# Conformer layer on one core: first weights ahead of x, a head first in the mixer, later half's norms in pieces, four one-pair weight blocks to a tile

## The chip, the cores and the metric

The kernel runs on one core of a Trainium2 chip. The metric is device time in microseconds of one execution, the median of several runs. The engines are named as the profile names them: PE is TensorE's matmuls, PEld its weight loads, DVE is VectorE, ACT is ScalarE, POOL is GpSimd and SP is SyncE, whose queue issues every DMA here. Each engine works through its own queue in order; a wait of one instruction holds up all behind it on that engine.

## The reference

One layer for 1,056 tokens (1,024 of a new stream and 32 of a running one), model width 1,024, in float32:

```
x = x + 0.5 * RMSNorm_post(SwiGLU_1(RMSNorm_pre(x)))
h = RMSNorm_pre(x); p = h @ w_in
conv group: GLU -> causal depthwise conv (width 31) -> LayerNorm -> swish
ret group:  rotary q,k -> chunkwise retention (4 heads of 128) -> GroupNorm -> * swish(g)
x = x + RMSNorm_post(concat(conv, ret) @ w_out)
x = x + 0.5 * RMSNorm_post(SwiGLU_2(RMSNorm_pre(x)))
```

The feed-forward width is 2,816; w_in has 3,072 columns (four convolution blocks of value and gate, four heads of q, k, v, g, 128 columns each). The outputs are y and the new convolution and retention states.

## The kernel before

**Arithmetic.** Each operand of a large product is split into a high part (rounded to fp32r) and a low part (the rest), and a product takes three matmuls: high by high, high by low, low by high. A weight split is one copy on ACT (L146, tile `whi`) and one subtraction, on POOL as a rule (L147, tile `wlo`). Tokens lie along the free axis in two halves of 528, each in two pieces of Q = 264; features lie on the 128 partitions. Pairs of feature blocks and token pieces form 2x2 block products. The feed-forwards mostly do these with seven block products in place of eight (`visit`, L305 to 348, matmul L323), with sums and differences of blocks as operands; elsewhere plain blocks are used (`visit_plain`, L266 to 303, matmul L275).

**Units.** `program` is a list of units. A unit is one block of weights with one or two visits (one for each half that uses it). `prep` (L156 to 208) is a generator for its weights: it fetches four blocks into `raw` tiles (five buffers), then forms sums and differences on DVE, then splits (seven buffers each of `whi` and `wlo`). `run` (L358 to 402) goes through the units; while the products of one are issued, it steps the generator of the next, and when a unit ends it issues the fetch of the unit after the next.

**Order.** There is a planned clock, `now`, which advances by 0.124 us for each large matmul issued (L278, L326). Side work is put into a heap with a due time (`later`, `at`), and is issued when the clock reaches it. Instructions that come out this way are then placed in the engines' queues by the tile framework, with a simulated timeline. So the constants on L49 to L58 set where norms, convolution taps and retention steps fall among the matmuls.

**Stages.** First the opening: vec, both halves of x (16 loads, L976), two constant tiles, and `begin(0)` (L983 to 989), which squares and sums x (`Norm`, L406 to 456), scales it (L475) and splits it. The first half's statistics are a matmul `sp` (L437), `v` on DVE (L440), a power on POOL (L441) and a matmul `bc` (L449); the squares go through one buffer, tag `sq` (L415). The feed-forward's up part (L524 to 597) follows: three pairs of units for the first half alone with plain blocks, three for the second half alone, and the rest for both. Hidden values are stored to DRAM in split form (L559, L560) and loaded again (L113) for the down part, which runs over five blocks of pairs, `DBLK` = 1, 2, 2, 2, 4 pairs; the first four use the kind `paired` with seven products, the last is plain, first half and then second.

**Kind `paired`** (L178 to 195). It puts two 128-column-by-nk blocks side by side into each of four `raw` tiles, so a unit has four fetches, four DVE operations and four splits. With nk = 1 the splits are 256, 256, 256 and 128 wide, with nk = 2 twice that.

**Between feed-forward and mixer.** After the last visit of a half, `post_norm` (L506 to 520) scales ys (L512), adds the residual (L513), stores, and starts the next `pre_norm` (L467 to 495), which scales again (L475) and splits (`tplain`, L242 to 248, DVE at L247). In both, all four pairs are issued in one go.

**Mixer.** Twenty-four plain units, twelve for a half: a convolution is one unit (`cu`), a head is two (`hu`: q and k, then v and g). The order in a half is c0, c1, h0, c2, h1, c3, h2, h3. A convolution's 31 taps are DVE instructions on 558 or 528 columns (L740, L742), one a planned us, and the four convolutions of a half queue behind each other. A head's q and k are multiplied by a cosine table out of PSUM (L836). Retention runs in five chunks a head and a half (`retain`, L856 to 925) with three steps each; `RET_DELAY` holds the delay from the first step to the second, from the second to the third, from the unit to the first chunk, and between chunks. Results of convolutions and heads go through DRAM (`cd`, `rd`), and `conv_norm` and `ret_build` make the operands of the out-projection from them, after the last unit of the half. Feed-forward hidden blocks (`h`), results (`ys`), convolutions (`cu`) and heads (`hd`) share four buffers, tag `f`. PSUM has four banks for large products: two `px`, one `py`, one `pz`. The out-projection has four plain units for the first half, then four for the second, and is followed by the second feed-forward.

Of the kernel before, what the change touches and what calls it, by code (L numbers as in the profile page):

```python
# [10 lines left out]
F32 = mybir.dt.float32  # L11
# [4 lines left out]
P = 128  # L16
# [34 lines left out]
TAP_STEP = 1.0  # L51
RET_DELAY = (4.0, 10.0, 4.0, 4.0)
NORM_DELAY = (2.0, 3.0)
BEGIN_DELAY = 2.0
SPILL_STEP = (1.4, 2.8, 5.6, 9.0)
# [9 lines left out]
def layer_kernel(ctx: ExitStack, tc: tile.TileContext, a: dict, o: dict):  # L65
# [90 lines left out]
    def prep(src, nk, kind, dve_lo):  # L156
# [20 lines left out]

        def paired():  # L178
            n = nk * P
            r = [raw() for _ in range(4)]  # L180
            a11, s1, a12, s2, s4, a22, s3 = (r[p // 2][:, p % 2 * n:p % 2 * n + n] for p in range(7))
            for t, i in ((a11, 0), (s3, 1), (a22, 2), (a12, 3)):
                fetch(t, src, i, nk)
            yield
            v = nc.vector
            v.tensor_tensor(s1, s3, a22, ALU.add)
            v.tensor_tensor(s2, s1, a11, ALU.subtract)
            v.tensor_tensor(s4, a12, s2, ALU.subtract)  # L188
            v.tensor_tensor(s3, a11, s3, ALU.subtract)
            yield  # L190
            for p in range(4):
                m = n if p == 3 else 2 * n
                hi, lo = split(r[p], m, p in dve_lo)
                ws.extend((hi[:, o:o + n], lo[:, o:o + n]) for o in range(0, m, n))
                yield
# [11 lines left out]

        return ws, {"seven": seven, "paired": paired, "plain": plain}[kind]()

# [147 lines left out]

    def run():  # L358

        made = [prep(s, nk, kind, dl) for s, nk, _, dl, kind in program]  # L360
        made.append(([], iter(())))
        next(made[0][1])
        for _ in made[0][1]:
            pass
        next(made[1][1])
        for n, (src, nk, visits, _, kind) in enumerate(program):
# [4 lines left out]
            if n + 1 < len(program):  # L371
                nkind = program[n + 1][4]
                pieces_ = {"seven": 7, "paired": 4, "plain": 4}[nkind]

                if nkind == kind == "seven":
                    plan = [max(0, total - 8 - (total > 7) * 3)] + [total - 7 + i for i in range(7)]
                else:
                    plan = [0] + [total - 1 - (pieces_ - 1 - i) * max(1, min(2, (total - 1) // pieces_)) for i in range(pieces_)]
            else:
                plan = []  # L380
# [25 lines left out]
    class Norm:  # L406
# [4 lines left out]

        def add(self, x, dt=0.0):

            def first():
                sq = fp.tile([P, 4, Q], F32, name=nm("sq"), tag="sq", bufs=1)  # L415
                nc.scalar.activation(sq, x, AF.Square)
# [49 lines left out]

    def pre_norm(j, bs, nrm, g, dst, also=None, plain=False, dt=NORM_DELAY, then=lambda: None):  # L467

        def done(rb):
            if also is not None:  # L470
                ex = [tp.tile([P, 4, Q], F32R, name=nm("ex"), tag=t) for t in ("tbh", "tbl")]
            rest = []
            for kp, b in enumerate(bs):
                for i, x in enumerate(pieces(b)):
                    nc.vector.scalar_tensor_tensor(x, x, col(g, 2 * kp + i), rb, ALU.mult, ALU.mult)  # L475
                if plain:
                    tplain(b, dst, j, kp)
                    continue
                if kp % 2 == 0:
# [25 lines left out]

    def post_norm(j, fs, nrm, xs, g, mul, out, gpre, dst, also=None, plain=False):  # L506

        def done(rb):
            n2 = Norm(4)
            for kp, b in enumerate(groups(fs)):  # L510
                for k, y in zip((2 * kp, 2 * kp + 1), pieces(b)):
# [3 lines left out]
                if gpre is not None:  # L515
                    n2.add(b, POST_STEP * (kp + 1))
            if gpre is not None:
                pre_norm(j, groups(fs), n2, gpre, dst, also if j == 0 else None, plain, NEXT_DELAY)

        nrm.finish(1.0 / D, mul, done)  # L520

    def ffn(xt, wgu, wdn, res, gpost, out, gpre, nxt, lead, first):  # L524
# [114 lines left out]
        for b, (k0, nk) in enumerate(DBLK):  # L639
            last = b == len(DBLK) - 1  # L640

            def dn_visit(m, j, before, b=b, last=last):
# [9 lines left out]
                def after():  # L652
                    if last:
# [4 lines left out]
                        if m == 3:  # L658
                            post_norm(j, ys[j], sums[j], xs[j], gpost, 0.5, out, gpre, nxt, None, True)

# [10 lines left out]
            if last:  # L671
                for j in (0, 1):
                    for m in range(4):
                        unit(src[m], nk, [dn_visit(m, j, None)], (), "plain")
            else:
                for m in range(4):
                    unit(src[m], nk, [dn_visit(m, j, start if m == j == 0 else None) for j in (0, 1)], (), "paired")

# [299 lines left out]

    inp = [[fetch_x(j, q) for q in (0, 1)] for j in (0, 1)]
    nc.sync.dma_start(out=idn, in_=a["idn"])  # L980
    nc.sync.dma_start(out=msk, in_=a["msk"])

    def begin(j):  # L983
        bs = groups(inp[j])
        nrm = Norm(4)
        for i, b in enumerate(bs):
            nrm.add(b, 0.0 if j == 0 else 2.0 * i)
        pre_norm(j, bs, nrm, "f1pre", xt[0], first[0] if j == 0 else None, False, (0.0, 0.0) if j == 0 else (10.0, 3.0),
                 (lambda: later(BEGIN_DELAY, lambda: begin(1))) if j == 0 else lambda: None)

    begin(0)
    ffn(xt[0], a["wgu1"], a["wd1"], a["x"], "f1post", x1, "mpre", xt[1], 3, first[0])
# [10 lines left out]
    for j in (0, 1):  # L1003
        cu(0, j)
        cu(1, j)
        hu(0, j)
        cu(2, j)
        hu(1, j)
        cu(3, j)
        hu(2, j)  # L1010
        hu(3, j)
        src, nk, ((b, tj, dst, acc, after),), dl, pl = program[-1]
# [7 lines left out]
    ffn(xt[3], a["wgu2"], a["wd2"], x2, "f2post", o["y"], None, None, 3, first[1])  # L1020
    run()
    flush()
# [65 lines left out]
```

## Time and profile before

| | |
|---|---|
| median of 3 runs | 2114.32 us (2112.15 to 2115.62) |
| the profiled execution | 2111.57 us, span of its instructions 2109.8 us |
| PE busy | 1927.7 us, 91% |
| DVE busy | 1441.4 us, 68% |
| POOL busy | 995.5 us, 47% |
| ACT busy | 825.8 us, 39% |
| HBM read and written | 217.54 MB and 88.50 MB, 145 GB/s over the span |
| TensorE's granted clock, mean | 0.974 |

How to read it: matmuls are pipelined and their ends are modelled, so a busy PE need not be at its peak; the count of matmuls in a stretch tells more. A row of waits gives who waited, for whom, the us in total, the number of waits and the longest. A row of groups gives line, engine, operation, tiles and shapes, then the busy time, the mean of one in ns, and the idle time before them with what ended it. The feed-forwards fill about 40 to 800 us and 1320 us to the end; the mixer lies between.

### The profile page before, as it was taken

To read this page: it belongs to the slowest core of one execution; us is meant where nothing else is said; L and a number is where in the kernel's file an instruction comes from. 1 tells how busy PE (TensorE), PEld (TensorE's weight loads), DVE (VectorE), ACT (ScalarE), POOL (GpSimd) and SP (SyncE) were. 2 spreads that over 40 slices of the span, in tenths; PEclk is the share of its full clock that TensorE was granted. 3 is DMA by queue.
4 is the path that set the end of the run, shared out by engine and by line. 5 is a ranking of instruction groups with operands and counts; after the bars stand their busy time and mean duration, and the time that the engine had idled before them with its cause. 6 is when DMAs were issued, how large, how long until landed. Compare 5 with 4: busy or idle time off the path is not lost. (4 is left out here: it accounts for less than half of the span.)

```text
span 2109.8 us, 39258 instructions
## 1 busy us (share of the span) xinstructions
PE 1927.7 (91%) x15272; PEld 1886.6 (89%) x15272; DVE 1441.4 (68%) x2386; ACT 825.8 (39%) x1564; POOL 995.5 (47%) x734
## 2 busy tenths in 40 slices
PE   4988999999899997589988999888999999999995
PEld 4988999999899997589988999887999999889995
DVE  7777566543677378989799855988676544477545
ACT  5444444444322233233433345444444444432221
POOL 2556544454354454354454446456554545344441
PEclk9999999999999999699999999999999999999998
DMA  4354434433975653032332354324444423676742
GB/s 146 104 175 146 141 117 151 135 102 122 329 256 165 214 163 113 23 94 87 105 104 80 99 188 130 127 81 163 140 157 155 135 86 130 233 256 222 254 142 83
DMA packets 143977, 308.60 MB, mean 146 GB/s; under 512 B 17456, under 2 KB 47536, under 8 KB 143792
## 3 DMA queue, kind: packets, MB, share of 16 engines
q1 hardware_dynamic: 143792, 306.10, 43.7%
q8 instruction: 120, 1.97, 0.4%
q14 instruction: 65, 0.53, 0.1%
HBM read 217.54 MB, written 88.50 MB: 145 GB/s over the span
## 5 line engine op out<-in xcount | busy, mean ns | idle before, releaser
L147 POOL TENSOR_TENSOR wlo<-raw,whi 128x512 fp32r<-128x512 f32 (+1 forms) x620 | 874.7, 1427 | 885.5 <-ACT whi L146 714.1
L146 ACT ACTIVATE whi<-raw 128x512 fp32r<-128x512 f32 (+1 forms) x632 | 366.3, 606 | 652.2 <-issue 178.1
L742 DVE SCALAR_TENSOR_TENSOR cu<-cu,vec 128x558 f32<-128x558 f32 (+1 forms) x240 | 242.9, 1032 | 1.6
L275 PE MATMUL px<-tbh,whi 128*128 128x264 f32 x768 | 225.9, 294 | 19.4 <-DVE hd L836 14.3
L323 PE MATMUL px<-tbh,whi 128*128 128x264 f32 x832 | 238.8, 287 | 3.1 <-ACT h L313 1.9
L323 PE MATMUL px<-tbh,wlo 128*128 128x264 f32 x832 | 237.2, 285 | 0.0
L323 PE MATMUL px<-tbl,whi 128*128 128x264 f32 x832 | 236.7, 284 | 0.0
L275 PE MATMUL px<-tbl,whi 128*128 128x264 f32 x768 | 221.5, 289 | 0.6 <-DVE tbl L247 0.6
L275 PE MATMUL px<-tbh,wlo 128*128 128x264 f32 x768 | 221.4, 288 | 0.0
L275 PEld LDWEIGHTS px<-tbh,whi 128*128 128x128 f32 x768 | 147.6, 192 | 20.3 <-issue 14.5
L323 PEld LDWEIGHTS px<-tbh,whi 128*128 128x128 f32 x832 | 157.2, 189 | 5.2 <-ACT h L313 2.8
L323 PEld LDWEIGHTS px<-tbh,wlo 128*128 128x128 f32 x832 | 157.3, 189 | 0.0
L323 PEld LDWEIGHTS px<-tbl,whi 128*128 128x128 f32 x832 | 157.2, 189 | 0.0
L275 PEld LDWEIGHTS px<-tbl,whi 128*128 128x128 f32 x768 | 147.1, 192 | 0.9 <-DVE tbl L247 0.9
L275 PEld LDWEIGHTS px<-tbh,wlo 128*128 128x128 f32 x768 | 147.1, 191 | 0.1
L316 DVE TENSOR_TENSOR h<-h,px 128x264 f32<-128x264 f32 x152 | 59.1, 424 | 117.1 <-PE px L323 109.7
L323 PE MATMUL px<-tah,whi 128*128 128x264 f32 x416 | 119.8, 288 | 14.2 <-ACT whi L146 13.3
L323 PE MATMUL py<-tbh,whi 128*128 128x264 f32 x416 | 121.9, 293 | 9.5 <-DVE h L316 7.6
L323 PE MATMUL pz<-tbh,whi 128*128 128x264 f32 x416 | 121.6, 292 | 8.1 <-DVE ys L316 3.3
L323 PE MATMUL pz<-tbl,whi 128*128 128x264 f32 x416 | 119.5, 287 | 7.1 <-DVE tbl L237 6.3
L323 PE MATMUL pz<-tah,wlo 128*128 128x264 f32 x416 | 119.8, 288 | 4.7 <-DVE wlo L147 2.9
L323 PE MATMUL py<-tah,whi 128*128 128x264 f32 x416 | 120.5, 290 | 2.7 <-ACT ys L313 1.0
(217 smaller groups left out, 6023.6 us busy)
## 6 DMA issues: line engine op xcount, KB each, us to landing
raw<-in_wgu SPq DMA_DIRECT2D x224, 256.0 KB, 3.3
hth<-hh SPq DMA_DIRECT2D x28, 924.0 KB, 4.0
htl<-hl SPq DMA_DIRECT2D x28, 924.0 KB, 5.0
raw<-in_win SPq DMA_DIRECT2D x96, 256.0 KB, 3.3
tbh<-hth SPq DMA_DIRECT2D x44, 528.0 KB, 5.6
tbl<-htl SPq DMA_DIRECT2D x44, 528.0 KB, 6.0
raw<-in_wd SPq DMA_DIRECT2D x64, 256.0 KB, 3.0
raw<-in_wd SPq DMA_DIRECT2D x96, 128.0 KB, 3.1
```

Source lines behind the costliest of these rows:

```text
L146: nc.scalar.activation(hi, x[:, :n], AF.Copy)
L147: (nc.vector if dve else nc.gpsimd).tensor_tensor(lo, x[:, :n], hi, ALU.subtract)
L275: mm = nc.tensor.matmul(ps, l[:, w], r, start=k == 0 and i == 0 and n == 0, stop=k == nk - 1 and i == 1 and n == 2)
L316: nc.vector.tensor_tensor(to, to, ps, ALU.add)
L323: mm = nc.tensor.matmul(ps, l[:, w], r, start=start and k == 0 and i == 0, stop=k == nk - 1 and i == 2, skip_group_check=True)
L742: nc.vector.scalar_tensor_tensor(cc, u[:, t:t + m], vec[:, w + t:w + t + 1], cc, ALU.mult, ALU.add)
```

## The change

1. **Opening.** x is no longer loaded before the program is built. `run` fetches the first unit's four weight blocks, then calls `opening`, which loads the first half of x and the identity, and puts two things into the heap: `begin(0)`, and after it `others`, which loads the second half of x and the mask. Between them the splits of the first unit and the fetch of the second unit are issued. `begin(0)` squares into two tiles of tag `g` instead of the single `sq` buffer. `BEGIN_DELAY`, from the first half's scaling to `begin(1)`, goes from 2 to 8.
2. **Packing.** `paired` becomes `packed`: 4 // nk blocks to a `raw` tile. For nk = 2 it is as before; for nk = 1 four blocks share a tile, so the seven fill two tiles and the splits are 512 and 384 wide.
3. **Mixer's order.** In the first half h0, c0, c1, h1, c2, h2, c3, h3; the second half is as before.
4. **Later half's norms.** Between the first feed-forward and the mixer, the second half's `post_norm` and `pre_norm` issue their four pairs `SPREAD` = 5 planned us apart, with delays of 4 and 4 in the first and 20 and 4 in the second.
5. **Retention.** `RET_DELAY` goes from (4, 10, 4, 4) to (6, 11, 4, 5).

```diff
-RET_DELAY = (4.0, 10.0, 4.0, 4.0)
+RET_DELAY = (6.0, 11.0, 4.0, 5.0)
+SPREAD = 5.0
-BEGIN_DELAY = 2.0
+BEGIN_DELAY = 8.0
...
-        def paired():
+        def packed():
             n = nk * P
-            r = [raw() for _ in range(4)]
-            a11, s1, a12, s2, s4, a22, s3 = (r[p // 2][:, p % 2 * n:p % 2 * n + n] for p in range(7))
+            per = 4 // nk
+            r = [raw() for _ in range((6 + per) // per)]
+            a11, s1, a12, s2, s4, a22, s3 = (r[p // per][:, p % per * n:p % per * n + n] for p in range(7))
...
-            for p in range(4):
-                m = n if p == 3 else 2 * n
-                hi, lo = split(r[p], m, p in dve_lo)
+            for p, x in enumerate(r):
+                m = min(per, 7 - p * per) * n
+                hi, lo = split(x, m, p in dve_lo)
...
-    def run():
+    def run(opening):
         made = [prep(s, nk, kind, dl) for s, nk, _, dl, kind in program]
         made.append(([], iter(())))
         next(made[0][1])
+        opening()
         for _ in made[0][1]:
             pass
         next(made[1][1])
...
-                pieces_ = {"seven": 7, "paired": 4, "plain": 4}[nkind]
+                pieces_ = {"seven": 7, "packed": (7 * program[n + 1][1] + 3) // 4, "plain": 4}[nkind]
...
     def pre_norm(...):
...
             for kp, b in enumerate(bs):
+                if slow:
+                    later(SPREAD * kp, lambda kp=kp, b=b: scaled(kp, b))
+                    continue
+                scaled(kp, b)
...
     def post_norm(...):
...
                 if gpre is not None:
-                    n2.add(b, POST_STEP * (kp + 1))
+                    n2.add(b, 1.5 if slow else POST_STEP * (kp + 1))
+            for kp, b in enumerate(groups(fs)):
+                if slow:
+                    later(SPREAD * kp, lambda kp=kp, b=b: pair(kp, b))
+                else:
+                    pair(kp, b)
             if gpre is not None:
-                pre_norm(j, groups(fs), n2, gpre, dst, also if j == 0 else None, plain, NEXT_DELAY)
-        nrm.finish(1.0 / D, mul, done)
+                pre_norm(j, groups(fs), n2, gpre, dst, also if j == 0 else None, plain,
+                         (4 * SPREAD, 4.0) if slow else NEXT_DELAY, slow=slow)
+        nrm.finish(1.0 / D, mul, done, (4.0, 4.0) if slow else NORM_DELAY)
...
-    inp = [[fetch_x(j, q) for q in (0, 1)] for j in (0, 1)]
-    nc.sync.dma_start(out=idn, in_=a["idn"])
-    nc.sync.dma_start(out=msk, in_=a["msk"])
+    inp = [None, None]
+    def opening():
+        inp[0] = [fetch_x(0, q) for q in (0, 1)]
+        nc.sync.dma_start(out=idn, in_=a["idn"])
+        at(0.0, lambda: begin(0))
+        at(0.0, others)
+    def others():
+        inp[1] = [fetch_x(1, q) for q in (0, 1)]
+        nc.sync.dma_start(out=msk, in_=a["msk"])
...
+        if j == 0:
+            sq = [gtile("sq"), gtile("sq")]
...
     for j in (0, 1):
-        cu(0, j)
-        cu(1, j)
-        hu(0, j)
-        cu(2, j)
-        hu(1, j)
-        cu(3, j)
-        hu(2, j)
-        hu(3, j)
+        for x in ("h0", "c0", "c1", "h1", "c2", "h2", "c3", "h3") if j == 0 else ("c0", "c1", "h0", "c2", "h1", "c3", "h2", "h3"):
+            (cu if x[0] == "c" else hu)(int(x[1]), j)
```

More of the change, by code (lines that the diff above doesn't have):

```diff
@@ L206, in plain @@
                 yield
-        return ws, {"seven": seven, "paired": paired, "plain": plain}[kind]()
+        return ws, {"seven": seven, "packed": packed, "plain": plain}[kind]()
     PART = ((0, 0), (1, 0), (0, 1), (1, 1), (0, 2), (1, 3), (1, 2))
@@ L410, in __init__, with add, first @@
             self.n, self.got = n, 0
-        def add(self, x, dt=0.0):
-            def first():
-                sq = fp.tile([P, 4, Q], F32, name=nm("sq"), tag="sq", bufs=1)
+        def add(self, x, dt=0.0, sq=None):
+            def first(sq=sq):
+                if sq is None:
+                    sq = fp.tile([P, 4, Q], F32, name=nm("sq"), tag="sq", bufs=1)
                 nc.scalar.activation(sq, x, AF.Square)
@@ L465, in groups, with pre_norm @@
         return [f[:, 4 * i:4 * i + 4] for f in fs for i in (0, 1)]
-    def pre_norm(j, bs, nrm, g, dst, also=None, plain=False, dt=NORM_DELAY, then=lambda: None):
+    def pre_norm(j, bs, nrm, g, dst, also=None, plain=False, dt=NORM_DELAY, then=lambda: None, slow=False):
         def done(rb):
@@ L472, in done, with scaled @@
             rest = []
-            for kp, b in enumerate(bs):
+            def scaled(kp, b):
                 for i, x in enumerate(pieces(b)):
@@ L477, in done @@
                     tplain(b, dst, j, kp)
+            for kp, b in enumerate(bs):
+                if slow:
+                    later(SPREAD * kp, lambda kp=kp, b=b: scaled(kp, b))
+                    continue
+                scaled(kp, b)
+                if plain:
                     continue
@@ L504, in residual, with post_norm, pair @@
         return xs
-    def post_norm(j, fs, nrm, xs, g, mul, out, gpre, dst, also=None, plain=False):
+    def post_norm(j, fs, nrm, xs, g, mul, out, gpre, dst, also=None, plain=False, slow=False):
         def done(rb):
             n2 = Norm(4)
-            for kp, b in enumerate(groups(fs)):
+            def pair(kp, b):
                 for k, y in zip((2 * kp, 2 * kp + 1), pieces(b)):
@@ L658, in after @@
                         if m == 3:
-                            post_norm(j, ys[j], sums[j], xs[j], gpost, 0.5, out, gpre, nxt, None, True)
+                            post_norm(j, ys[j], sums[j], xs[j], gpost, 0.5, out, gpre, nxt, None, True, j == 1 and gpre is not None)
                 return (before, hts[b][j], evict if last else dst, not last and b > 0, after)
@@ L676, in ffn @@
                 for m in range(4):
-                    unit(src[m], nk, [dn_visit(m, j, start if m == j == 0 else None) for j in (0, 1)], (), "paired")
+                    unit(src[m], nk, [dn_visit(m, j, start if m == j == 0 else None) for j in (0, 1)], (), "packed")
     def mixer(xt, wt):
@@ L985, in begin @@
         nrm = Norm(4)
+        if j == 0:
+            sq = [gtile("sq"), gtile("sq")]
         for i, b in enumerate(bs):
-            nrm.add(b, 0.0 if j == 0 else 2.0 * i)
+            nrm.add(b, 0.0 if j == 0 else 2.0 * i, sq[i // 2][:, 4 * (i % 2):4 * (i % 2) + 4] if j == 0 else None)
         pre_norm(j, bs, nrm, "f1pre", xt[0], first[0] if j == 0 else None, False, (0.0, 0.0) if j == 0 else (10.0, 3.0),
                  (lambda: later(BEGIN_DELAY, lambda: begin(1))) if j == 0 else lambda: None)
-    begin(0)
     ffn(xt[0], a["wgu1"], a["wd1"], a["x"], "f1post", x1, "mpre", xt[1], 3, first[0])
@@ L1020, in layer_kernel @@
     ffn(xt[3], a["wgu2"], a["wd2"], x2, "f2post", o["y"], None, None, 3, first[1])
-    run()
+    run(opening)
     flush()
```

## The prediction

> **What bounds the kernel now.** I read the page first, then TensorE's waits, then a table of windows.
>
> ```profile
> span 2109.8 us, 39258 instructions
> PE 1927.7 (91%) x15272; PEld 1886.6 (89%) x15272; DVE 1441.4 (68%) x2386; ACT 825.8 (39%) x1564; POOL 995.5 (47%) x734
> ```
> ```profile
> PE sp L437 <- DVE ss L420: 36.3, 5, 16.1
> PE px L275 <- DVE hd L836: 14.3, 1, 14.3
> PE px L323 <- ACT whi L146: 13.3, 9, 2.9
> PE pz L275 <- DVE ex L485: 8.3, 2, 5.7
> ```
> ```profile
> 500.00:525.00 25.00, 25.00 (x208) 25.00 (x207) 8.31 (x18) 11.50 (x24) 10.94 (x9) 1.00 0.33 107
> 25.00:50.00 25.00, 15.82 (x109) 14.93 (x110) 25.00 (x38) 11.37 (x17) 6.06 (x4) 1.00 0.17 58
> 525.00:575.00 50.00, 42.73 (x308) 39.88 (x308) 29.90 (x74) 21.87 (x57) 19.36 (x23) 0.97 0.89 316
> 825.00:875.00 50.00, 17.54 (x120) 16.86 (x120) 50.00 (x69) 15.67 (x24) 14.00 (x8) 0.66 0.27 87
> 800.00:1212.00 412.00, 351.97 (x2738) 341.07 (x2738) 376.31 (x628) 148.93 (x316) 187.24 (x143) 0.93 0.29 88
> 1018.00:1212.00 194.00, 175.19 (x1372) 169.72 (x1371) 183.55 (x324) 74.57 (x161) 90.05 (x70) 0.96 0.31 91
> 1825.00:1875.00 50.00, 41.96 (x305) 39.13 (x304) 30.69 (x77) 20.65 (x53) 17.10 (x20) 0.97 0.88 323
> ```
>
> After the length, the columns are PE, PEld, DVE, ACT and POOL with counts, then TensorE's clock, DMA share and GB/s. TensorE is the bound almost everywhere: 208 matmuls in 25 us, 0.120 us each, is its full rate. It falls short in the opening (109 in 25 us), in each feed-forward's one-pair blocks (308 and 305 in 50 us, against 416), and where the mixer begins (120 in 50 us). In the mixer's projections, 800 to 1212, VectorE is busy 376 of 412 us, so there are nearly two bounds at once. The change reaches all four places. Where TensorE is the bound on both sides of a stall, what is taken out of the stall goes into the end time.
>
> **The opening.** DMA rates of the first 60 us in 40 slices of 1.5 us, then instructions from the timeline (start, length, engine, line, what it did, and in brackets the idle time before it and what ended that):
>
> ```profile
> GB/s 0 131 334 306 374 394 372 371 367 366 371 388 138 0 15 160 171 178 157 161 153 154 75 0 0 0 0 0 0 11 0 0 0 0 0 141 40 86 203 214
> ```
> ```profile
> x<-in_x SPq DMA_DIRECT2D x16, 264.0 KB, 5.3
> ```
> ```profile
> 13.50 1.08 ACT L416 ACTIVATE sq<-x 128x1056 f32<-128x1056 f32 x1 [1.57 <-DVE ss L420]
> 16.13 1.92 PE L437 MATMUL sp<-one,ss 128*88 128x1 f32 x12 [16.13 <-DVE ss L420]
> 19.63 11.43 POOL L147 TENSOR_TENSOR wlo<-raw,whi 128x512 fp32r<-128x512 f32 x7
> 24.78 9.56 DVE L475 SCALAR_TENSOR_TENSOR x<-x,vec,ss 128x528 f32<-128x528 f32 x8
> 35.70 0.59 PE L275 MATMUL pz<-ex,whi 128*128 128x264 f32 x1 [5.70 <-DVE ex L485]
> 859.67 5.51 DVE L475 SCALAR_TENSOR_TENSOR ys<-ys,vec,ss 128x528 f32<-128x528 f32 x8
> ```
>
> One square buffer makes ACT and DVE take turns: 1.08 + 1.57 = 2.65 us a round, until the sum is ready at 16.13. Two tiles with four halves end the turns, but four weight loads of 256 KB (1.05 MB at the row's 372 GB/s, 2.8 us) now go ahead of x. By that row the first 2.3 MB, which hold the first half of x (8 x 264 KB), are in by 9.0 us, so now by about 12; a square (1.08), its adds (about 1.5) and landing follow: the sum at about 15, a gain of 1. The larger part is the scaling, L475: 9.56 us beside the POOL splits that start at 19.63, and 5.51 for the same eight instructions near 860. With weights first, these splits run while x lands, so 4 us go. The second half's squares and adds, now queued behind, no longer sit ahead of the scaling: 1 more. So the first dense matmuls move from 35.7 to about 29.7: **-6**. Bounds: -2 if the next unit's splits still meet the scaling, -9 if the 5.70 us wait for the low part shrinks as well. The second half of x is moved behind the second unit's weights on SP's queue, whose issues wait for raw buffers. Its reader is the first seven-product unit, six units (6 x 96 x 0.120 = 69 us) later: that cover pays for it, and for a beginning of the second half that is 6 us later (BEGIN_DELAY).
>
> **One-pair blocks.** The waits of TensorE in 520 to 600 and in 1822 to 1900, SP's own wait in 1822 to 1880, and the splits by shape:
>
> ```profile
> PE px L323 <- ACT whi L146: 4.3, 3, 2.3
> PE px L323 <- ACT whi L146: 5.5, 3, 2.9
> SPq L154 <- DVE raw L189: 8.8, 4, 4.0
> L147 POOL TENSOR_TENSOR wlo<-raw,whi 128x256 fp32r<-128x256 f32 x14 | 11.2, 815 | 33.4 <-ACT whi L146 33.4
> L147 POOL TENSOR_TENSOR wlo<-raw,whi 128x512 fp32r<-128x512 f32 x6 | 8.2, 1395 | 6.3 <-ACT whi L146 5.2 <-PE pz L323 1.0
> ```
>
> A unit has 42 matmuls, 5.0 us, and takes four of five raw buffers, so its successor's loads wait until they are free. With two buffers a unit the successor's loads go out while it runs. The splits fall from four to two: 3 x 0.815 and a smaller one become 1.395 and a smaller one, about 0.6 us of POOL less a unit, off the path. At most 4.3 + 5.5 = 9.8 us go, 12 with the low clock behind such stops (0.97 in both windows). But DMA is 0.89 and 0.88 busy there, and what is late next is the stored hidden values of the next block on the same queue, or the first, longer split (+0.58). I take about 60%: **-6** (0 to -12).
>
> **The mixer's beginning.**
>
> ```profile
> 851.20 1.92 PE L437 MATMUL sp<-one,ss 128*88 128x1 f32 x12 [14.94 <-DVE ss L420]
> 856.00 2.87 PE L449 MATMUL bc<-idn,r 88*128 88x88 f32 x12 [2.88 <-POOL r L441]
> 873.18 0.56 PE L275 MATMUL px<-tbh,whi 128*128 128x264 f32 x1 [14.31 <-DVE hd L836]
> ```
> ```profile
> 853.99 5.76 DVE L742 SCALAR_TENSOR_TENSOR cu<-cu,vec 128x558 f32<-128x558 f32 x8
> 870.74 1.25 DVE L247 TENSOR_TENSOR tbl<-ys,tbh 128x1056 fp32r<-128x1056 f32 x1
> 872.62 0.42 DVE L836 TENSOR_TENSOR hd<-px,cos 128x264 f32<-128x264 f32 x1
> 893.74 6.90 DVE L742 SCALAR_TENSOR_TENSOR cu<-cu,vec 128x558 f32<-128x558 f32 x4
> ```
> ```profile
> L742 DVE SCALAR_TENSOR_TENSOR cu<-cu,vec 128x558 f32<-128x558 f32 (+1 forms) x240 | 242.9, 1032 | 1.6
> ```
> ```profile
> 893.12 6.91 POOL L147 TENSOR_TENSOR wlo<-raw,whi 128x512 fp32r<-128x512 f32 x4
> 1000.00:1025.00 25.00, 25.00 (x205) 24.41 (x204) 15.48 (x42) 10.46 (x25) 12.20 (x12) 1.00 0.39 117
> 1212.00:1262.00 50.00, 50.00 (x421) 49.87 (x419) 28.86 (x69) 26.13 (x51) 24.07 (x21) 1.00 0.60 196
> ```
>
> TensorE stands 14.94 + 2.88 + 14.31 = 32.1 us, and about 3 more go to the low clock (0.66): 35. Both long waits have one cause, the later half's norms among convolution taps. First its statistics come late; then the head's tile (third of four in tag "f", after two convolutions) can only be had when the last of that half's ys is read (870.74), and L836 follows at 872.62. Now a head comes first, with no taps, and the third tile is asked for after three units, 34.6 us. By the constants the norms, five us apart, free their tiles 37 and 47 us after they begin, and a unit can fill four banks, 11.5 us, before its tile must be there. I expect at most a few us of this stop to stay. What is moved with it: the first head issues its cosine and sine loads a unit after the norms instead of three units later, and the same 11.5 us of banks cover their landing; the later half's eight output stores are spread with its pairs, and each waits on SP for VectorE ahead of weight loads that are needed one unit, 11.5 us, later. Both at nothing; without that cover a late load would cost what it lacks, which the bounds below hold.
>
> What is left is VectorE's work, of which nothing is removed. It was idle 412 - 376 = 36 us. By the constants (96 x 0.124 = 11.9 a unit) the first half's 124 taps ran from 11.9 to 135.9 of 142.8; now from 35.7 to 159.7, so 17 taps pass into the second half. They fill the hole between the halves (idle 25 - 15.5 = 9.5 us at 1000 to 1025). Another 12 us can lag past 1212, where VectorE works 29 of 50 us. So 9.5 + 12 = 21.5: **-22**, and 390 us for this stage. Bounds: -35, the whole stop, and 0, where the taps take it all back. The longer retention delays (+2, +1, +1 a chunk) take small waits off TensorE here, and where VectorE is the bound that is worth nothing. I leave them at 0, within the bounds.
>
> **The mixer's end.** The last head, and the window after it:
>
> ```profile
> 1256.21 0.33 DVE L916 SCALAR_TENSOR_TENSOR hd<-rp,vec,hd 128x105 f32<-128x105 f32 x1 [3.46 <-PE rp L914]
> 1266.25 1.26 DVE L247 TENSOR_TENSOR tbl<-rf,tbh 128x1056 fp32r<-128x1056 f32 x1 [3.13 <-ACT tbh L246]
> 1250.00:1300.00 50.00, 50.00 (x418) 50.00 (x418) 22.31 (x31) 22.44 (x42) 28.70 (x17) 1.00 0.38 117
> ```
>
> The last chunk's third step is planned at 4 + 4x4 + 4 + 10 = 34 us and now at 4 + 4x5 + 6 + 11 = 41. From that step to the last operand is 1267.5 - 1256.2 = 11.3 us, through memory and back. The out-projection's first half lasts 4 x 11.5 = 46 us, and no wait shows: the operand came just in time. Seven us later leaves a wait of 7 less some 3 of slack: **+5** with the low clock after it (0 to +9).
>
> **Sum:** -6 - 6 - 22 + 5 = -29; 2111.57 - 29 = 2082.6. The profiled execution is 2111.57 (span 2109.8), 2.7 below the runs' median of 2114.32; by that median, 2085.
>
> **A page and a row.** Four taps beside POOL took 6.90 us, 1.73 each, against 5.76 / 8 = 0.72 where POOL does no splits. The Trainium skill, "SBUF — State Buffer", section "SBUF: two separate sides", says VectorE and GpSimd share a port pair as an exclusive lock, and the loser fully blocks. The trace agrees (1.73 against 0.72), and the rule speaks against this change: the first rival below is what it would do.
>
> **Rivals.** *VectorE takes it back.* During TensorE's stop POOL had no splits to make, and taps ran at 0.72. If TensorE does not stop, POOL does not either: some 30 taps that ran alone meet splits, at up to 1.73 each, 30 x 1.0 = 30 us, and the 22 is gone: -6 - 6 + 5 = -7, 2107. For it: VectorE at 50.00 of 50 in 825 to 875. Against: its 36 us of idle time, and POOL's work (187 us) is the same.
>
> *TensorE alone is the bound.* The whole stop goes and retention is in time: -6 - 6 - 35 = -47, 2067. For it: 352 busy of 412. Against: 183.55 of 194 for VectorE in the second half.
>
> *Slower: the carried taps.* 17 taps at their mean of 1.03 are 17.5 us in a second half that has 194 - 183.6 = 10.4 idle; convolution tiles come free later and heads hold theirs 7 us longer, so each new unit waits for a tile. If none of that is hidden, the first half gives nothing, blocks give 0 and the opening -2: +17 + 9 - 2 = +24, 2138. It decides from where the first half gives back less than these 26.
>
> *Not what it says:* the blocks stay bound by DMA, 6 less; inside the range.
>
> **Numbers.** Forecast 0.60, VectorE takes it back 0.20, TensorE alone 0.12, slower 0.08. The range reaches from all bounds at their best (-9 - 12 - 35 = -56: 2058) to just above the first rival, 2109. About 0.2% (4 us) is what a measurement can tell from no change: within it 0.05, taken from the first rival; faster 0.87, slower 0.08.
>
> **What would show it.** The first dense matmul near 30 and L475 near 5.5 us; no wait of px for whi above 1 us in the one-pair blocks; L836 no longer after the last tbl<-ys, and no wait of sp above 5 us near 800 to 850; the projections in about 390 us with VectorE over 95% busy; a new wait of a few us at the out-projection's second half. A projection stage of 410 us, or waits for tiles in the second half, would prove it wrong.

## The result and the profile after

Four runs of the changed kernel gave a median of 2093.01 us (2090.26 to 2097.97), and four of the kernel before 2114.97 us (2112.15 to 2118.70). The ratio is 0.9898 (95% interval 0.9873 to 0.9922): 22 us less, where 29 were forecast. The profiled execution after is the one of 2090.26 us; by it the gain over the profiled one before (2111.57) is 21.3.

The page of the kernel after, its head and one row of groups (busy us, mean ns of one, idle before):

```profile
span 2088.4 us, 39191 instructions
PE 1931.3 (92%) x15272; PEld 1889.8 (90%) x15272; DVE 1431.8 (69%) x2386; ACT 824.4 (39%) x1550; POOL 1003.0 (48%) x718
L762 DVE SCALAR_TENSOR_TENSOR cu<-cu,vec 128x558 f32<-128x558 f32 (+1 forms) x240 | 239.6, 1017 | 1.0
```

Work on the engines has hardly changed (PE +3.6, DVE -9.6, POOL +7.5 us), so the gain is idle time. Lines have moved by 1 to 20: L742, the taps, is now L762, L836 is L856, L275 is L277.

Both kernels issue the same 14,496 large matmuls in the same units (in another order in the mixer), so a matmul of the same number can be timed in both traces. Differences between the start times of numbered matmuls cut the run into stages:

```
stage, us                     before   after   change
start to 25th matmul            40.0    36.7    -3.3
rest of FF1 up part            490.6   488.9    -1.7
FF1 one-pair block              31.4    24.4    -7.0
FF1 next block                  45.6    50.9    +5.3
rest of FF1 down part          182.9   183.5    +0.6
mixer, first half              223.6   196.4   -27.2
mixer, second half             197.4   208.2   +10.8
out-projection, first half      57.0    58.1    +1.1
out-projection, second half     51.4    53.5    +2.1
FF2 up part                    508.0   507.8    -0.2
FF2 one-pair block              32.1    24.4    -7.7
FF2 next block                  44.6    49.9    +5.3
rest of FF2 down part          181.0   181.2    +0.2
last large matmul at          2085.6  2064.0   -21.6
```

The one-pair blocks and the mixer's first half win much, and the stage behind each gives part of it back. That is the pattern to explain.

**Opening.** After, from the timeline:

```profile
15.30 4.26 POOL L148 TENSOR_TENSOR wlo<-raw,whi 128x512 fp32r<-128x512 f32 x3 [4.65 <-ACT whi L147]
15.55 1.66 DVE L424 TENSOR_TENSOR ss<-ss,sq 128x528 f32<-128x528 f32 x1
13.62 1.08 ACT L420 ACTIVATE sq<-x 128x1056 f32<-128x1056 f32 x1 [0.41 <-DMA x<-in_x]
17.26 1.92 PE L441 MATMUL sp<-one,ss 128*88 128x1 f32 x12 [17.26 <-DVE ss L424]
25.00 5.52 DVE L480 SCALAR_TENSOR_TENSOR x<-x,vec,ss 128x528 f32<-128x528 f32 x8
31.88 0.59 PE L277 MATMUL pz<-ex,whi 128*128 128x264 f32 x1 [3.67 <-DVE ex L497]
```

The scaling takes 5.52 us in place of 9.56, as forecast, and the first dense matmul comes at 31.88 in place of 35.70. But the sum is ready at 17.26, later than before (16.13). The squares no longer take turns with the adds, but now wait for x, which comes later: the last one begins at 13.62, no sooner than before (13.50). And the last add takes 1.66 us beside the POOL splits that begin at 15.30, where adds alone take 0.71.

**One-pair blocks.** After, TensorE's waits in 525 to 602, and windows for the one-pair block and the next (PE, PEld, DVE, ACT, POOL, clock, DMA share, GB/s); then the same two windows before:

```profile
PE px L325 <- ACT whi L147: 2.0, 1, 2.0
```
```profile
525.60:549.90 24.30, 22.19 (x169) 20.98 (x168) 17.24 (x46) 14.53 (x37) 4.49 (x4) 1.00 1.01 364
549.90:600.90 51.00, 46.91 (x337) 44.66 (x338) 37.36 (x86) 11.65 (x21) 25.32 (x21) 0.93 0.69 232
```
```profile
530.60:562.00 31.40, 25.37 (x169) 22.87 (x169) 18.52 (x49) 16.43 (x45) 8.42 (x13) 0.95 0.95 344
562.00:607.60 45.60, 42.46 (x339) 41.27 (x338) 36.60 (x86) 12.02 (x22) 24.85 (x22) 1.00 0.68 234
```

The 168 large matmuls of the one-pair block (the windows cut into one more) take 7 us less and its waits for weights are gone. One such wait has moved into the next block, where the clock now drops to 0.93.

**Mixer.** TensorE's largest waits in 780 to 1200, and the place of the second of them:

```profile
PE uo L906 <- DVE on L929: 10.7, 7, 6.8
PE px L277 <- ACT cu L727: 6.1, 1, 6.1
PE px L277 <- DVE ys L670: 4.8, 1, 4.8
```
```profile
855.23 0.59 PE L277 MATMUL px<-tbh,whi 128*128 128x264 f32 x1 [6.13 <-ACT cu L727]
```

The waits of 14.94, 2.88 and 14.31 us are gone; 6.13 is left where they stood. The wait for ys (L670) was there before, 4.8 as well. Now windows of the halves. First the kernel before, all engines and then VectorE on the taps alone; then the same two of the kernel after:

```profile
790.50:1014.00 223.50, 176.90 (x1352) 170.96 (x1351) 200.06 (x312) 78.07 (x159) 97.89 (x74) 0.89 0.27 81
1014.00:1211.40 197.40, 178.59 (x1400) 173.12 (x1399) 185.56 (x327) 76.67 (x164) 92.48 (x71) 0.97 0.31 94
```
```profile
790.50:1014.00 223.50, 120.05 (x120) 0.89 0.27 81
1014.00:1211.40 197.40, 122.86 (x120) 0.97 0.31 94
```
```profile
784.40:980.80 196.40, 174.71 (x1360) 167.99 (x1359) 184.83 (x294) 77.29 (x159) 98.92 (x73) 0.96 0.30 89
980.80:1189.00 208.20, 181.35 (x1383) 176.51 (x1382) 194.13 (x338) 77.94 (x164) 96.13 (x71) 0.93 0.31 91
```
```profile
784.40:980.80 196.40, 102.26 (x102) 0.96 0.30 89
980.80:1189.00 208.20, 137.37 (x138) 0.93 0.31 91
1189.00:1300.00 111.00, 0.00 (x0) 1.00 0.50 159
```

Eighteen taps have passed from the first half into the second (138 against 120), 14.5 us of VectorE's time, and not one lies behind 1189. VectorE is idle 25.6 us of the two halves, where it was 35.3.

### The profile page after: what moved, and what is told of

The parts are those of the page before. It is cut to its first block, busy times and chain, and to the rows that moved or that the text cites. A ratio compares the mean times of both kernels' runs of the same rounds, so it can differ in the third digit from the quotient of the medians.

```text
span 2088.4 us, 39191 instructions
## 1 busy us (share of the span) xinstructions
PE 1931.3 (92%) x15272; PEld 1889.8 (90%) x15272; DVE 1431.8 (69%) x2386; ACT 824.4 (39%) x1550; POOL 1003.0 (48%) x718
## 5 line engine op out<-in xcount | busy, mean ns | idle before, releaser
L148 POOL TENSOR_TENSOR wlo<-raw,whi 128x512 fp32r<-128x512 f32 x604 | 875.4, 1465 | 847.8 <-ACT whi L147 686.0
L147 ACT ACTIVATE whi<-raw 128x512 fp32r<-128x512 f32 x616 | 363.5, 617 | 647.7 <-issue 172.7
L762 DVE SCALAR_TENSOR_TENSOR cu<-cu,vec 128x558 f32<-128x558 f32 (+1 forms) x240 | 239.6, 1017 | 1.0
L277 PE MATMUL px<-tbh,whi 128*128 128x264 f32 x768 | 226.4, 295 | 11.3 <-ACT cu L727 6.1
L277 PE MATMUL px<-tbl,whi 128*128 128x264 f32 x768 | 223.7, 291 | 0.6 <-DVE tbl L249 0.6
L277 PE MATMUL px<-tbh,wlo 128*128 128x264 f32 x768 | 222.4, 290 | 0.0
L277 PEld LDWEIGHTS px<-tbh,whi 128*128 128x128 f32 x768 | 149.3, 194 | 12.3 <-ACT cu L727 6.3
L277 PEld LDWEIGHTS px<-tbl,whi 128*128 128x128 f32 x768 | 148.6, 194 | 1.2 <-DVE tbl L249 0.9
L277 PEld LDWEIGHTS px<-tbh,wlo 128*128 128x128 f32 x768 | 148.5, 193 | 0.2 <-issue 0.2
```

The costliest lines, as they stand in the source:

```text
L147: nc.scalar.activation(hi, x[:, :n], AF.Copy)
L148: (nc.vector if dve else nc.gpsimd).tensor_tensor(lo, x[:, :n], hi, ALU.subtract)
L277: mm = nc.tensor.matmul(ps, l[:, w], r, start=k == 0 and i == 0 and n == 0, stop=k == nk - 1 and i == 1 and n == 2)
L762: nc.vector.scalar_tensor_tensor(cc, u[:, t:t + m], vec[:, w + t:w + t + 1], cc, ALU.mult, ALU.add)
```

## The experiments

Theory A: VectorE's throughput bounds the second half, so the taps that are carried into it come back as TensorE's time. Theory B, the rival: the second half and the out-projection are longer because of the longer retention delays. For the blocks: the weights of the next block lie behind the loads of stored hidden values (C), against too few buffers or slow splits. All stages of the runs, cut as above (one profiled execution each; kernels with the same code in a mixer half still differ there by up to 4 us, u9's first half by 8, since the queues are laid anew for each):

```
             opening FF1lead1 blk1+2 mix1  mix2  out1 out2 FF2blk1+2  last
before        40.0    86.8    77.0  223.6 197.4  57.0 51.4   76.7   2085.6
after         36.7    80.9    75.3  196.4 208.2  58.1 53.5   74.3   2064.0
u1            36.7    81.0    73.7  199.9 206.0  59.5 53.6   73.4   2064.0
u2            37.5    80.9    73.9  219.8 197.9  58.1 55.1   73.8   2078.6
u3            36.8    80.9    73.7  196.1 203.7  57.0 51.4   73.7   2056.2
w3            37.4    80.9    74.0  195.6 203.7  57.0 51.4   74.9   2056.8
u5            37.9    81.0    73.5  197.9 185.4  58.1 56.6   73.4   2042.2
u10           35.9    80.9    73.7  210.1 197.9  57.0 51.6   75.6   2064.2
u6            39.6    80.3    72.3  196.6 205.0  59.5 55.1   74.0   2061.4
u7            36.8    80.6    74.3  196.4 207.6  58.1 56.7   75.3   2065.5
u12           36.4    84.3    73.9  196.8 207.2  58.1 55.1   74.0   2066.3
u9            36.3    80.9    69.4  204.5 203.9  59.4 55.0   69.3   2058.4
v1            36.5    80.9    69.6  196.9 205.9  57.0 51.6   69.2   2047.9
v2            36.8    81.0    69.7  197.3 202.7  57.0 51.4   68.3   2044.8
```

FF1lead1 runs from the first large matmul to the 577th, the first half's six units with plain blocks; it overlaps the opening, which ends at the 25th. blk1+2 is the one-pair block and the next. Kernels without an interval ran once, beside the kernel before at 2112.87 to 2115.52.

**u2_convs_first: the old order in the mixer.**

```diff
-        for x in (...) if j == 0 else ("c0", "c1", "h0", "c2", "h1", "c3", "h2", "h3"):
+        for x in (...) if False else ("c0", "c1", "h0", "c2", "h1", "c3", "h2", "h3"):
```

> The changed kernel with the first half's units in the old order (c0, c1, h0, ...), norms still spread. If the order removed the stop, the wait for the head's tile comes back and the first half is near 220 us, and the second half, which then gets no carried taps, goes from 208 back to about 197: total about 2102. If the spreading alone is enough, the first half stays near 196 and the second falls to 197: total about 2080, better than the changed kernel.

2104.59 us. The stop is back in the first half (219.8), and the second half is as short as before (197.9). Its timeline:

```profile
843.77 1.92 PE L441 MATMUL sp<-one,ss 128*88 128x1 f32 x12 [12.97 <-DVE ss L424]
865.75 0.56 PE L277 MATMUL px<-tbh,whi 128*128 128x264 f32 x1 [14.31 <-DVE hd L856]
```

Both waits are back, though the plan issues the norms in pieces here. So the head that goes first removes the stop, and the same edit lengthens the second half.

**u1_norms_at_once: the later half's norms in one go, a head first.**

```diff
-  post_norm(j, ys[j], sums[j], xs[j], gpost, 0.5, out, gpre, nxt, None, True, j == 1 and gpre is not None)
+  post_norm(j, ys[j], sums[j], xs[j], gpost, 0.5, out, gpre, nxt, None, True)
```

> The changed kernel with the later half's norms issued all at once again, a head still first. The projections take 404.6 us in the changed kernel (196.4 and 208.2 by halves) and 420.9 before (223.5 and 197.4). If the head's place alone removed the stop of TensorE (no taps among the norms), the first half stays within 5 us of 196. If the spreading did it, eight scalings and eight adds in one lump hold up the head's evictions, and the first half grows by 10 us or more. Total 2090 or 2100.

2090.80 us, beside 2090.26: the halves are 199.9 + 206.0 = 405.9 against 404.6. Spreading the norms is worth nothing that these traces can tell; the prediction credited order and pieces together. In fact the pieces did not stay apart. The plan issues the scalings of `pre_norm` in pairs 5 us apart, but in the changed kernel VectorE makes all eight in one run, as in u1 (first the changed kernel, then u1):

```profile
843.52 6.52 DVE L480 SCALAR_TENSOR_TENSOR ys<-ys,vec,ss 128x528 f32<-128x528 f32 x8
839.14 5.52 DVE L480 SCALAR_TENSOR_TENSOR ys<-ys,vec,ss 128x528 f32<-128x528 f32 x8
```

What norms that really come in pieces would be worth is not shown.

**u5_half_taps: fewer taps.** In the second half only 16 of 31 taps are made; the kernel leaves 15 taps of that half's four convolutions out (60 in all).

```diff
-            if t + 1 < CW:
+            if t + 1 < (CW if j == 0 else 16):
```

> The changed kernel with 16 of 31 convolution taps in the second half of the tokens (the other 15 are left out, so that half's convolution is another one); 4 x 15 taps at 1.02 us are 61 us of VectorE. If VectorE's throughput is the bound of the second half (theory A), it falls from 208 us to near TensorE's own busy time there, 181, so by 20 to 27 us. If late steps of retention and held tiles are what holds TensorE (theory B), it falls by less than 10.

2068.26 us. The second half, 981.10 to 1166.50, is 22.8 us shorter:

```profile
981.10:1166.50 185.40, 172.79 (x1382) 169.87 (x1382) 144.10 (x278) 78.33 (x164) 86.79 (x71) 0.97 0.33 102
```

With 144 of 185 us busy VectorE no longer sets the pace, and TensorE's 172.79 remain. Some 59 us of taps (78 in this half in place of 138) are thus worth 22.8. This is what theory A says, and theory B does not: the longer delays are still in this kernel.

**u3_ret_old and w3_ret_old_timed: the old retention delays.** The same kernel twice, the second time timed.

```diff
-RET_DELAY = (6.0, 11.0, 4.0, 5.0)
+RET_DELAY = (4.0, 10.0, 4.0, 4.0)
```

> The changed kernel with the old retention delays (4, 10, 4, 4). Theory A (VectorE's carried taps make the second half longer): the second half stays within 3 us of 208. Theory B (heads hold their tiles 7 us longer and the steps come late): it falls to about 198, and the total to about 2081. In both, the out-projection's second half begins 1 to 3 us sooner after its first half.

> The changed kernel with the old retention delays, timed. One run gave 2083.0 against 2090 to 2098 for the changed kernel. If the delays cost 7 us, the ratio to the kernel before is near 0.985 and its interval lies below 0.9898; if the one run was luck, it is near 0.990.

Once it took 2083.03; timed, the median is 2082.22 us (2080.24 to 2082.83, four runs), ratio 0.9852 (0.9837 to 0.9867), outside the interval of the change (0.9873 to 0.9922). The longer delays cost about 8 us: 7.2 by the last matmul of the traces of w3 and after, 10.8 by the medians. Some 4.5 of it lie in the second half (203.7 in both traces), which is no more than kernels scatter there: u9 has 203.9 with the new delays, v1 205.9 with the old. The out-projection is firm: with the old delays it takes 108.4 to 108.6 in the five kernels that have them and in the kernel before, with the new ones 111.6 to 114.8 in all eight. So B holds for the out-projection, and for the second half it is likely but not shown.

In w3, second half, 979 to 1183, TensorE waits directly for retention more than after (9.5 us in three such waits there):

```profile
PE uo L906 <- DVE on L929: 17.1, 6, 6.9
```

The longer delays did shorten these waits, and the stage was longer all the same. It is VectorE that stands idle longer. Its second half in w3 (columns as above):

```profile
979.50:1183.20 203.70, 178.56 (x1392) 174.13 (x1392) 196.81 (x344) 75.44 (x164) 102.36 (x73) 0.94 0.31 94
```

VectorE is idle for 6.9 us there and for 14.1 after. In the four kernels with the old delays and this order it is 6.9 to 8.4 us, in the six with the new delays and all taps 8.7 to 14.1. Its largest waits there are for ACT's `vt` of a retention step (L890), 4.5 us after and 0.8 in w3, and for the load of `cd` (L812), 2.5 and none. Why the longer delays bring these waits is open.

**u10_conv_head_conv: a convolution first, then a head, with the old delays.** An attempt to keep the VectorE queue fed.

```diff
-RET_DELAY = (6.0, 11.0, 4.0, 5.0)
+RET_DELAY = (4.0, 10.0, 4.0, 4.0)
...
-        for x in ("h0", "c0", "c1", "h1", "c2", "h2", "c3", "h3") if j == 0 else (...):
+        for x in ("c0", "h0", "c1", "c2", "h1", "c3", "h2", "h3") if j == 0 else (...):
```

> The changed kernel with the old retention delays and the first half's order c0, h0, c1, c2, h1, c3, h2, h3, to be compared with the run that has the old delays alone (196.1 and 203.7 us by halves, 2083). The third tile is still asked for after three units, but the taps begin a unit after the start, and by the constants end at 140.6 of 142.8: none is carried over. If the carried taps cost the second half its time, it falls from 203.7 to about 198, and the first half grows by 3 us or less: total about 2079. If taps among the norms bring the stop back, the first half grows by 10 us or more.

2090.23 us, 7 more than u3. Only one tap is carried (121 in the second half), and the second half is back at 197.9; but the stop is back in part, and the first half takes 210.1:

```profile
PE px L277 <- ACT cu L727: 9.9, 1, 9.9
...
PE sp L441 <- DVE ss L424: 5.9, 1, 5.9
```

With u2 it shows both sides of the trade: 0 or 1 carried taps and 197.9, or 15 to 21 and 202.7 to 208.2, in every kernel that makes all taps. By u3 (141 taps there) and u10, both with the old delays, 20 carried taps cost 5.8; by the change and u2, both with the new delays, 18 cost 10.3.

**u6_one_square, u7_x_first, u12_begin_2: the opening.** One square buffer; x fetched ahead of the first unit's weights; the second half's beginning 2 after the first half's scaling.

```diff
 u6
-            sq = [gtile("sq"), gtile("sq")]
+            sq = None
-        nrm.add(b, 0.0 if j == 0 else 2.0 * i, sq[i // 2][...] if j == 0 else None)
+        nrm.add(b, 0.0 if j == 0 else 2.0 * i, None)
 u7
-        next(made[0][1])
         opening()
+        next(made[0][1])
 u12
-BEGIN_DELAY = 8.0
+BEGIN_DELAY = 2.0
```

> The changed kernel with the single square buffer in the opening. If the two square tiles matter, ACT and DVE take turns again (2.65 us a round) behind an x that lands 2.8 us later, the sum is ready near 18 instead of 15, and the first unit's end (36.7 us after the start for the 25th matmul) moves later by 2 to 3 us. If the arrival of x paces them anyway, nothing moves by more than 0.5 us.

> The changed kernel with the first half of x ahead of the first unit's weights on SP's queue (the second half of x stays behind the second unit's weights). If the gain of the opening (6.6 us) comes from POOL's splits being out of the way of the scaling L475, the scaling goes back toward 9.6 us for eight and 3 to 4 us of the gain are lost. If it comes from the second half's squares and adds being behind, the splits don't matter, x lands 2.8 us sooner, and the start is up to 2 us earlier than in the changed kernel.

> The changed kernel with the second half's beginning 2 instead of 8 planned us behind the first half's scaling. In the kernel before, VectorE's evictions of the first units waited for that half's work (2.6 and 0.8 us), and the six units of the first half took 86.8 us; in the changed kernel 80.9. If the later beginning removed those waits, they come back and the six units take about 84; if the shorter opening did, they stay at 81.

2087.76, 2091.51 and 2092.23 us. The opening is read from the timelines, since a few us come and go in the mixer (u6 is ahead of the changed kernel at the end by what it has less there and in the blocks). u6, then u7:

```profile
21.11 1.92 PE L441 MATMUL sp<-one,ss 128*88 128x1 f32 x12 [21.11 <-DVE ss L424]
35.35 0.59 PE L277 MATMUL pz<-ex,whi 128*128 128x264 f32 x1 [4.02 <-DVE ex L497]
```
```profile
11.94 7.39 POOL L148 TENSOR_TENSOR wlo<-raw,whi 128x512 fp32r<-128x512 f32 x5 [11.50 <-DMA raw<-in_wgu]
14.13 1.92 PE L441 MATMUL sp<-one,ss 128*88 128x1 f32 x12 [14.13 <-DVE ss L424]
24.33 6.53 DVE L480 SCALAR_TENSOR_TENSOR x<-x,vec,ss 128x528 f32<-128x528 f32 x8
32.22 0.59 PE L277 MATMUL pz<-ex,whi 128*128 128x264 f32 x1 [3.67 <-DVE ex L497]
```

With one buffer the sum is 3.9 us later and the first dense matmul 3.5 later (35.35 against 31.88): the two square tiles are the gain. With x first the sum is ready 3.1 us earlier, but the power on POOL stands behind five splits until 19.33, and the scaling takes 6.53: the first dense matmul is 0.3 later. Weights ahead of x are worth next to nothing: what the scaling gains by them, the later x gives back. u12 shows the rest: with the old `BEGIN_DELAY` the first half's six units take 84.3 in place of 80.9 (86.8 before), and TensorE waits there for VectorE's hidden values, in 36 to 110:

```profile
PE py L277 <- DVE h L601: 1.9, 1, 1.9
```

**u9_loads_spread: stored values asked for later.** While a block runs, the down part plans the loads of the next block's hidden values. It spreads them over 6.5 in place of 5 times the length of one visit: 33.9 planned us in place of 26.0 in a block with nk = 2, 16.9 in place of 16.0 with nk = 1.

```diff
-                    build(b + 1, 8 - 2 * nk, max(5 * us, 16.0), 7 * us)
+                    build(b + 1, 8 - 2 * nk, max(6.5 * us, 16.0), 7 * us)
```

> The changed kernel with the loads of the next block's stored hidden values spread over 6.5 instead of 5 unit lengths (factor 5 * us to 6.5 * us). The one-pair block gained 7.0 us and the next block gave 5.3 back, with a wait for whi of 2.0 us and a low clock behind it; its weight loads were issued at 567 to 569 and landed at 574 to 576 among the stored values' loads. If those loads hold the weights up, the second block falls from 51 to about 45 us in each feed-forward and the total by about 10. If the raw buffers alone do, nothing moves by more than 1 us.

2084.35 us. First the kernel after: the issues on SP's queue, the wait that follows, and how long weights took to land in 567 to 576 (KB each, us from issue to landing):

```profile
567.11 0.68 SPq L155 DMA_DIRECT2D raw<-in_wd  x1
568.27 0.32 SPq L114 DMA_DIRECT2D tal<-htl  x1
568.68 0.62 SPq L155 DMA_DIRECT2D raw<-in_wd  x1
```
```profile
574.85 2.21 ACT L147 ACTIVATE whi<-raw 128x512 fp32r<-128x512 f32 x4 [9.69 <-DVE raw L188]
```
```profile
tbl<-htl SPq DMA_DIRECT2D x1, 528.0 KB, 7.5
...
raw<-in_wd SPq DMA_DIRECT2D x2, 128.0 KB, 7.1
```

A weight block a quarter as large as a load of stored values took as long to land as those around it, 7.1 us, where the kernel's 128 KB loads take 3.5 as a median; the DMA engines were busy for 0.87 of this window. In u9 the same windows read

```profile
525.60:549.90 24.30, 21.79 (x166) 20.59 (x165) 18.49 (x46) 14.19 (x37) 5.89 (x5) 1.00 1.00 367
549.90:600.90 51.00, 49.55 (x390) 47.72 (x389) 39.22 (x94) 12.53 (x23) 26.56 (x22) 1.00 0.72 242
```

and the next block takes 44.6 in place of 50.9, in both feed-forwards (44.5 against 49.9). C is shown: the loads held the weights up, with the buffers and the splits as they were. The gain in the blocks is 5.9 + 5.0 against the changed kernel, whose blocks are among the longest: the ten kernels with its loads have 146.3 to 149.6 for both pairs together, the three with spread loads 138.0 to 138.8, so it is 8 to 12 us. It did not all reach the end, since the mixer's first half took 204.5 in this trace; v1 with the same edit took 196.9, so that is not the edit's doing alone, and why stays open.

**v1_ret_old_spread and v2_tap0_on_act: the better versions.** v1 is u3 and u9 together. v2 is v1 with the first tap of each convolution on ACT, which was 39% busy:

```diff
-                nc.vector.tensor_scalar(cc, u[:, 0:m], vec[:, w:w + 1], col("cb", i), ALU.mult, ALU.add)
+                nc.scalar.activation(cc, u[:, 0:m], AF.Identity, scale=vec[:, w:w + 1], bias=col("cb", i))
```

> The changed kernel with the two edits that gained alone: old retention delays (2083 in one run) and the stored values' loads spread over 6.5 units (2084 in one run). If they add, the blocks give 11 us and the delays 7: 2090 - 18 = 2072 to 2076. Spreading the loads alone made the mixer's first half 8 us longer for a reason not known; if that comes with it again, about 2080. The ratio to the kernel before should then be 0.980 to 0.984, below the changed kernel's interval of 0.9873 to 0.9922.

> The run before this with the first of 31 taps (scale and bias, eight instructions) on ACT instead of VectorE. If VectorE's throughput bounds the projections, 8 x 1.0 us less work there gives 4 to 8 us. If what is left is the order of the steps in the queues, nothing is gained, and a tap that waits in ACT's queue ahead of evictions can cost a few us.

v1: 2072.81 us (2072.73 to 2074.61, five runs), ratio 0.9811 (0.9796 to 0.9825). v2: 2069.44 us (2067.38 to 2071.77, four runs), ratio 0.9794 (0.9777 to 0.9810). Both beat both kernels. The gains add: 8 from the delays and 6 from u9 make 14 of the 17 between the change's profiled time and v1. v2's 3 us over v1 fits theory A (eight VectorE operations fewer), but their intervals just overlap.

## Why the prediction came out as it did

The forecast of 2085 was 8 us too good, inside its range, and of the four terms none was more than 6 off. By the stage table, against the forecast:

**Opening: -6 forecast, -6.6 measured.** (Up to the 577th matmul, where the second half's lead begins: 113.8 before, 107.2 after; 1.6 of them are lost again in the rest of the up part.) That the size came out is luck, for the working was only half right. The -6 was worked out for the first dense matmul, and that moved by 3.8. Scaling gained its 4, but the later x took as much back (u7); the two square tiles, put at 1, are worth 3.5 there (u6). The sum was to be at 15 and came at 17.26: x was taken to be in by about 12, and the last square got its x at 13.62; and the last add, which has two inputs, took 1.66 in place of 0.71 beside the new splits. The prediction laid those splits beside x's landing and did not ask what VectorE does there. What made up for it is the longer `BEGIN_DELAY`, put down at nothing and worth 3.4 by the 577th matmul (u12): with the short delay the second half's adds and scaling lie among the first products' own work on VectorE. By the end of the up part 1.9 of it are left (527.5 in u12 against 525.6).

**One-pair blocks: -6 forecast, -1.7 and -2.5 measured.** In the one-pair blocks themselves it is -7.0 and -7.7, beyond the bound of -12. The prediction named what would be late next, the stored values of the next block on the same queue. It was the next unit's weights behind those loads, and it cost 5.3 each time, more than was allowed for. With the loads spread (u9) the two pairs of blocks are 7.6 and 7.4 shorter than before, and the blocks right after them 1.6 and 1.4 longer: 12.0 in all.

**Mixer's beginning: -22 forecast, -16.3 measured.** The first half gained 27.2, by the head alone (u2, u1). A few us of the stop stayed, as expected: 6.13. 17 taps were to be carried, and 18 were. The step that failed is "Another 12 us can lag past 1212": no tap lies behind the end of the projections, the last ended 6.4 us ahead of it (9.4 before), and VectorE works 29.1 of the 50 us behind it, where it worked 28.5. So of VectorE's 35.3 idle us only 9.7 were used, and not 21.5. The last convolution ends before the last heads, whose retention is VectorE's work too; at the end there is nothing to lag. The stage as cut here took 404.6, where -22 would be 399 (the forecast's 390 is for its window of 412 us, this stage took 420.9 before). The other step that failed is the retention delays ("I leave them at 0"), which cost about 8 us here and in the out-projection (w3). With the old ones the stage takes 399.3, and VectorE is idle for 18.4 of it; no tap lags there either. So without the delays the -22 would have come true in size, but not by work that lags.

**Mixer's end: +5 forecast, +3.2 measured, for another reason.** The operand did come 7 us later:

```profile
L249 DVE TENSOR_TENSOR tbl<-rf,tbh x2: 1258/1258/1258, 1245.1 to 1250.7; 128x1056 fp32r<-128x1056 f32 x2
```

It ends at 1252.0, 63.0 us after the out-projection began, against 56.1 before (1267.5 less 1211.4). So the shift was as forecast. TensorE did not wait for it: the framework's placing had changed as well, and three quarters of the first two blocks of the second half stood ahead of the products that need it. What waited is the statistics, in 1186 to 1302:

```profile
PE sp L441 <- DVE ss L424: 1.9, 1, 1.9
```

This wait is in each of the eight kernels with the new delays, and in none of the five with the old ones, nor before. It lies in the second half and makes most of its +2.1; the first half's +1.1 goes with 11 more small matmuls of retention that fall into it.

**The rivals.** *VectorE takes it back* had taps at up to 1.73 us as POOL no longer stops: the mean tap is 1017 ns, 1032 before, so the price did not rise. VectorE did take 10.8 of 27.2 back, by number of taps and not by their price: without carried taps (u2) 10.3 of the 10.8 are gone. *TensorE alone* would have needed a second half that does not grow. *Slower* had the carried taps at 17 and their sign right; they cost 5.8 (u10 against u3) to 10.3 (the change against u2) and not 17, since VectorE had idle time for the rest. That a wait for tiles would come on top was not seen.

## What to carry to other kernels

When a stall goes and the work that filled it on another engine does not, count that work as carried into the next stage, and credit the other engine's idle time only where it has something to do there: here 9.7 of 35.3 us were used, and 16.9 with the old delays. Behind a block that a queue bounded, look at the next block's share of the same queue before booking the gain; the packing alone gained 4 to 7 us in these blocks, spreading the bulk loads another 8 to 12. A delay that takes waits off one engine can cost more than the waits: test such constants alone.

## What the hardware showed

**A tap of 3.10 us.** Near 1086, from VectorE's, POOL's and PE's timelines of the kernel after:

```profile
1086.21 3.10 DVE L762 SCALAR_TENSOR_TENSOR cu<-cu,vec 128x528 f32<-128x528 f32 x1
1089.41 0.75 DVE L762 SCALAR_TENSOR_TENSOR cu<-cu,vec 128x528 f32<-128x528 f32 x1
```
```profile
1086.25 2.50 POOL L148 TENSOR_TENSOR wlo<-raw,whi 128x512 fp32r<-128x512 f32 x2
```
```profile
1090.63 0.77 PE L906 MATMUL uo<-vt,kt 106*128 106x128 f32 x2 [6.81 <-DVE on L929]
```

A tap that takes 0.75 alone was held for the length of two splits, and the longest wait of TensorE for retention, 6.81, ends behind it. The prediction took 1.73 as the most that a tap costs beside POOL.

**The clock after short waits.** In the kernel after, TensorE stood 2.03 us (573.5 to 575.5). Six matmuls later, at 576.5, its clock fell to half and stayed there until 583.3. A second stop of 0.62 us (576.5 to 577.2) lies in this slow stretch, not ahead of it:

```profile
575.00:576.50 1.50, 0.96 (x6) 0.79 (x6) 0.96 (x3) 1.38 (x3) 0.94 (x1) 0.99 0.12 48
576.50:580.00 3.50, 2.88 (x14) 2.85 (x14) 0.86 (x2) 0.56 (x2) 3.50 (x4) 0.50 0.48 132
580.00:583.40 3.40, 3.40 (x17) 3.40 (x17) 1.42 (x4) 0.00 (x0) 0.25 (x1) 0.51 0.93 290
```

TensorE was busy for 6.28 of these 6.9 us. At half rate that costs about 3.1, an estimate, which is more than the waits of 2.65. The Trainium skill, "TensorE: Matmul & The Clock Gate", section "What's actually happening", has the half clock after at least one idle window of about 3.4 us. The slow stretch, 6.8 us, is twice that window; but no idle stretch here was longer than 2.03 us, so in this trace 2.03 idle of the 3.4 us before the fall were enough.
